# FFN block products on plain activations that accumulate in PSUM, three of seven with both activation parts in one product

## The chip, the core and the metric

The kernel runs on one core of one Trainium2 chip. Its time is the device time of one execution in microseconds (us); lower is better. The core has TensorE (PE in the profile; its weight loads are PEld), VectorE (DVE), ScalarE (ACT), GpSimd (POOL), SyncE (SP) and 16 DMA engines. Matmul results land in PSUM, a buffer of 8 banks of 512 fp32 columns on 128 partitions.

## The reference

A trunk of two residual layers on x, 512 frames by 1024 channels in fp32. Each layer is FFN, mixer, FFN; the first layer's mixer is an SSD and S5 pair, the second's a band attention and a pooling. The FFNs are most of the work:

```python
h = _rmsnorm(x, ffn1_norm[layer])
x = x + 0.5 * _swiglu(h, ffn1_w_gate[layer], ffn1_w_up[layer], ffn1_w_down[layer])

def _rmsnorm(x, gain):
    y = xf * lax.rsqrt(jnp.mean(xf * xf, axis=-1, keepdims=True) + EPS)
    return (y * gain)
def _swiglu(h, w_gate, w_up, w_down):
    return (jax.nn.silu(h @ w_gate) * (h @ w_up)) @ w_down
```

`w_gate` and `w_up` are 1024 by 2816, `w_down` is 2816 by 1024.

## The kernel before

**Stages.** f0 (FFN), even (SSD and S5), f1 (FFN), f2 (FFN), odd (attention and pooling), f3 (FFN), in this order, on one core. Activations lie transposed: 8 tiles of 128 channels by 512 frames.

**Products.** Every operand is split in two parts of a reduced fp32 format (`fp32r`): a high part, and the rest. A product is three matmuls: high weights by high activations, high weights by low activations, low weights by high activations. `split` makes a high part by a cast on ScalarE and a low part by a subtraction on VectorE. The tiles are `raw` (weights as loaded, 128x1024), `whl` (both parts of 1024 columns), `wh` (both parts of 512 columns), `hg` (both parts of 512 frames of activations).

**An FFN's gate and up products.** The 2816 hidden channels are 11 pairs q of two 128-channel tiles. Up to a limit (`CLASSIC`: q = 9 in f0, q = 3 in the others) they are classic: for each tile 8 products of 512 frames, on activations that are multiplied by the norm's gain only; the norm's factor per frame (`rsB`) is multiplied in when the result is taken out of PSUM (`evac`). From the limit on, `pair` makes the two tiles of gate (i = 0) or of up (i = 1) with seven block products instead of eight, after Strassen and Winograd. The frames are halved (columns 0 to 255 and 256 to 511), the channels that are summed over are halved, and the two tiles are the halves of the output. A block product is four steps of 128 channels, each three matmuls of 256 columns. Its inputs are blocks of weights (W1, which holds two, W3 with two sums, W4 with two sums, W2), and blocks of activations: N, the normalised ones, and TA and TB, sums and differences of them. `blocks` prepares these once per FFN: it normalises (`normed`), forms four sums per step, splits them, then normalises again and splits N in the place of the plain activations. `HOLD` says how many are kept in between. PE may not start the first pair before all of N and TB are there.

**`pair` before.** X takes two block products of W1 in its two halves, Y two of W3, Z two of W4, V one of W2; each half is a group of its own. ScalarE copies one half of X out (tile `p`), VectorE joins the seven with seven additions of 256 columns into `gs` (gate) or `us` (up), with intermediate sums in `u`.

**What follows.** Silu on ScalarE, gate times up on VectorE, split (`gate`), then the down products: units ("wdn") of 24 matmuls of 512 columns in four PSUM banks, added to x at the end of each of the four groups of q (`GROUPS`).

**The order of the work.** It is fixed when the program is written. `ffn_items` lists pairs and down units: a group's down units are spread between the next group's pairs, except that at the limit `LEAD` of them come first (3 in f1 to f3, 4 in f0; tables of two numbers stand in this order). A clock that models each engine (`Clock`) goes along; generators (the weight feeder, `evac`, `gate`, `blocks`, and in f0 the S5 preparation `s5_prepare`) are asked after each step of PE whether they are due, in an order of priority (`PRIO`), and issue an instruction once `on` finds its inputs due and the engine's backlog small. For PE, `SLACK` asks that inputs be ready some time earlier. `side` picks a PSUM buffer that the clock takes to be free. Semaphores make the engines wait for one another on the chip, whatever the clock said. Each engine runs its own instructions in the order written.

**Buffers.** Weight loads go through SyncE's queue into 3 `raw` buffers, and 3 more from the time when the S5 preparation is over; the pairs have 5 `whl` and 2 `wh`. PSUM has 4 buffers for projections and pairs (`b`) and 4 for down units (`a`).

Of the kernel before, what the change touches and what calls it, by code (L numbers as in the profile page):

```python
# [17 lines left out]
P = 128  # L18
# [23 lines left out]
CLASSIC = (3, 9)  # L42
LEAD = (3, 4)
HOLD = (1, 0)
# [11 lines left out]
PRIO = {"evac": 0, "gate": 0, "small": 5, "prep": 6, "blocks": 6, "s5_bounce": 1, "s5_quarter": 0, "s5_gate": 0, "s5_eighth": 1,  # L56
# [52 lines left out]
class Clock:  # L109
# [140 lines left out]
class Builder:  # L250
    def __init__(self, ctx, tc, A, out, plan):
# [18 lines left out]
        self.f, self.rsB, self.h, self.ndone, self.reserve, self.then, self.final = None, None, None, 0, 0, None, False  # L270
        self.xhold, self.go = False, False
# [24 lines left out]
    def add(self, kind, gen):  # L296
        p = PRIO[kind]
        i = next((i for i, (q, _) in enumerate(self.threads) if q >= p), len(self.threads))
# [19 lines left out]
    def on(self, eng, *aps, ps=0):  # L318
        c = self.clk
        while True:  # L320
            r = c.ready(*aps)
            if eng == "PE":
                ok = r + SLACK[self.name] <= c.now
# [4 lines left out]
            if ok and (not ps or self.side(ps) is not None):  # L328
                return
# [27 lines left out]
    def side(self, n=1):  # L357
# [387 lines left out]
    def ffn(self, f, gi, then, prepare=None):  # L745
# [4 lines left out]
        with ExitStack() as st:  # L750
# [7 lines left out]
            def extra():  # L758
# [4 lines left out]
                self.xhold, self.go = prep is None, False  # L763
# [3 lines left out]
            self.N, self.TA, self.TB, self.ndone = h, [], [], 0  # L767
            grown = False
            for key in ffn_items(f):
# [3 lines left out]
                if key[0] == "blocks":  # L773
# [4 lines left out]
                    self.go = True  # L778
# [20 lines left out]
                elif key[0] == "pair":  # L799
                    q, i = key[2:]  # L800
                    self.until(lambda: self.ndone == KD and len(self.TB) == 4)
                    if i == 0:
                        t = {"gs": self.pair(w, "gs")}
                        nc.scalar.activation(out=t["gs"], in_=t["gs"], func=AF.Silu)
                    else:
                        t["us"] = self.pair(w, "us")
                        self.add("gate", self.gate(t, g, q, [1] * 4, 1))
                        if q == NFF // 2 - 1:
                            self.give(*self.N, *self.TA, *self.TB)
                else:  # L810
# [8 lines left out]
                    if cg == 1:  # L819
                        self.give(g[2 * kp], g[2 * kp + 1])  # L820
            if grown:
# [16 lines left out]
    def evac(self, ps, t, tag, m, done):  # L838
        while not self.scaled():
            yield  # L840
        if t[tag] is None:
            yield from self.room(tag, 1)
            if t[tag] is None:
                t[tag] = self.ft.tile([P, 2, S], F32, tag=tag, name=self.n(tag), bufs=1)
            else:
                self.leave(tag)
# [22 lines left out]
    def blocks(self, h, gi, late):  # L869
# [5 lines left out]

        hold = HOLD[late]
        again, kept = range(max(0, 4 - hold)), {}

        def normalized(kk, tag):
            t = yield from self.grab(tag, F32)  # L880
            n = (t[:, 0], t[:, 1]) if tag == "hg" else (t[:, lo], t[:, hi])
            for i in range(2):
                yield from self.normed(n[i], 4 * i + kk, h, gi, late)
            return t, n

        for kk in range(4):
            tn, (n1, n2) = yield from normalized(kk, "raw" if kk in again else "hg")
# [7 lines left out]
            v.tensor_tensor(out=t4, in0=t2, in1=n2[:, a], op=ALU.subtract)  # L895
            if kk in again:
                self.give(tn)
            else:
                kept[kk] = tn, (n1, n2)
# [4 lines left out]
            self.give(rt)  # L904

        for kk in again[:2]:
# [1184 lines left out]
```

## Time and profile before

| | |
|---|---|
| median of 3 runs | 1813.72 us (1812.3 to 1814.33) |
| the profiled execution | 1810.71 us, its span 1808.7 us |
| mean granted TensorE clock | 0.999 |
| PE busy | 1792.4 us (99%) |
| DVE busy | 1428.9 us (79%) |
| ACT busy | 754.7 us (42%) |
| HBM read | 192.82 MB |

Nearly every instruction is recorded under one line of the kernel, that of a helper, so the rows are told apart by tiles: `ps<-hg,whl` is a matmul of activations and weights into PSUM. With 128x512 it is a classic or a down product, with 128x256 one of a block. `whl<-raw,whl` on DVE is the second half of a weight split. A row of a window gives, after its length, the busy us of PE, PEld, DVE, ACT and POOL with their instructions, then the granted clock, the DMA engines' busy share and GB/s. A row of a group gives busy us and the mean ns of one, then the engine's idle time before them and what ended it. The stages lie at: f0 from 0 to about 385 us, even to about 540, f1 and f2 to about 1245, odd to about 1405, f3 to the end.

### The profile page before, as it was taken

How to read it: one execution, taken by the hardware profiler on the slowest of the kernel's cores; microseconds unless marked ns; L12 is line 12 of the kernel's file. 1: busy time of each engine (PE TensorE's matmuls, PEld its weight loads, DVE VectorE, ACT ScalarE, POOL GpSimd, SP SyncE). 2: the span in 40 equal slices, each digit the busy share in tenths (PEclk: the TensorE clock that was granted, in tenths of full speed). 3: DMA queues.
4: the chain of work that ended last, by engine and by line, in shares of the span. 5: the costliest groups of instructions: out<-in, count | busy, mean ns of one | idle time of the engine just before them, and what ended most of it. 6: DMA issues, size and time to landing. Idle time of an engine off the chain costs nothing.

```text
span 1808.7 us, 26795 instructions
## 1 busy us (share of the span) xinstructions
PE 1792.4 (99%) x10514; PEld 1564.3 (86%) x10514; DVE 1428.9 (79%) x2599; ACT 754.7 (42%) x1082; POOL 18.7 (1%) x35
## 2 busy tenths in 40 slices
PE   9999999999999999999999999999999999999999
PEld 7877888978878889999988999998888788999997
DVE  8989877878986878887777988775578678988864
ACT  4323423433574444343343444333466544434331
POOL 0000000000010000000000000000000000000000
PEclk9999999999999999999999999999999999999999
DMA  5247432337773223332422333332434422333331
GB/s 196 92 141 190 144 103 82 117 130 205 201 168 114 88 89 104 118 105 95 138 64 78 106 117 97 103 102 86 144 78 111 129 82 76 100 106 107 111 98 70
DMA packets 80749, 207.16 MB, mean 115 GB/s; under 512 B 18000, under 2 KB 30320, under 8 KB 79472
## 3 DMA queue, kind: packets, MB, share of 16 engines
q1 hardware_dynamic: 78032, 196.52, 34.6%
q0 software_dynamic: 2448, 8.91, 3.1%
q8 instruction: 83, 1.36, 0.3%
q14 instruction: 42, 0.34, 0.1%
q10 hardware_dynamic: 144, 0.02, 0.0%
HBM read 192.82 MB, written 12.60 MB: 114 GB/s over the span
## 4 chain that ended last, share of the span: by engine, by line
PE 88%; DVE 8%; DMA 2%; issue 1%; ACT 1%; SPq 0%; DVEq 0%; ACTq 0%
PE ps L205 88%; DVE whl L205 1%; DVE hg L205 1%; DVE us L205 1%; DVE ex L205 1%; DVE ssb L205 1%; DMA raw<-in_wglu_dram 0%; DMA prm<-prm 0%; DMA s5ys<-ys 0%; ACT whl L205 0%; DVE s5x L205 0%; DMA ssb<-acsd 0%; DVE sc L205 0%; ACT hg L205 0%; DMA raw<-in_wgu_dram 0%
## 5 line engine op out<-in xcount | busy, mean ns | idle before, releaser
L205 PE MATMUL ps<-hg,whl 128*128 128x512 f32 (+1 forms) x8688 | 1609.6, 345 | 5.5 <-DVE hg L205 2.5
L205 PEld LDWEIGHTS ps<-hg,whl 128*128 128x128 f32 x8688 | 1375.5, 190 | 203.8 <-issue 4.6
L205 ACT CAST whl<-raw 128x1024 fp32r<-128x1024 f32 x366 | 383.0, 1051 | 532.3 <-PE ps L205 323.4
L205 DVE TENSOR_TENSOR whl<-raw,whl 128x1024 fp32r<-128x1024 f32 x349 | 424.1, 1222 | 180.8 <-ACT whl L205 180.3
L205 DVE SCALAR_TENSOR_TENSOR x<-ps,x 128x512 f32<-128x512 f32 x128 | 87.1, 688 | 37.0 <-PE ps L205 35.4
L205 DVE TENSOR_TENSOR raw<-raw,raw 128x512 f32<-128x512 f32 (+1 forms) x182 | 111.3, 649 | 2.2
L205 ACT CAST hg<-us 128x512 fp32r<-128x512 f32 x88 | 52.1, 620 | 105.2 <-DVE us L205 104.9
L205 PE MATMUL ps<-hg,wh 128*128 128x256 f32 x624 | 83.4, 283 | 0.0
L205 ACT ACTIVATE gs<-gs 128x1024 f32<-128x1024 f32 x44 | 46.7, 1060 | 85.5 <-DVE gs L205 85.5
L205 PEld LDWEIGHTS ps<-hg,wh 128*128 128x128 f32 x624 | 78.6, 192 | 0.0
L205 DVE TENSOR_TENSOR raw<-raw 128x512 f32<-128x512 f32 (+1 forms) x78 | 46.6, 597 | 16.4 <-DMA raw<-in_wgu_dram 16.4
L205 ACT COPY p<-ps 128x256 f32<-128x256 f32 x52 | 19.3, 372 | 95.5 <-PE ps L205 86.1
L205 DVE TENSOR_TENSOR hg<-us,hg 128x512 fp32r<-128x512 f32 x88 | 57.9, 685 | 0.0
L205 DVE TENSOR_TENSOR us<-gs,us 128x1024 f32<-128x1024 f32 x44 | 53.6, 1219 | 0.4
L205 ACT ACTIVATE hg<-x,gains 128x512 fp32r<-128x512 f32 x48 | 33.6, 722 | 32.4 <-DVE x L205 30.0
L205 ACT CAST hg<-raw 128x512 fp32r<-128x512 f32 x58 | 34.4, 622 | 21.3 <-DVE raw L205 20.6
L205 DVE TENSOR_TENSOR hg<-raw,hg 128x512 fp32r<-128x512 f32 x58 | 38.1, 689 | 0.1
L205 DVE SCALAR_TENSOR_TENSOR hg<-x,gains,hg 128x512 fp32r<-128x512 f32 x48 | 34.9, 746 | 2.5 <-ACT hg L205 2.5
L205 DVE TENSOR_TENSOR wh<-raw,wh 128x512 fp32r<-128x512 f32 x52 | 35.7, 686 | 0.0
L205 DVE TENSOR_TENSOR us<-ps,rsB 128x512 f32<-128x512 f32 x40 | 28.9, 723 | 4.5 <-PE ps L205 4.4
L205 ACT CAST wh<-raw 128x512 fp32r<-128x512 f32 x52 | 32.0, 616 | 0.0
L205 DVE TENSOR_TENSOR acc<-acc,sq 128x512 f32<-128x512 f32 x42 | 29.0, 690 | 0.9
(264 smaller groups left out, 1100.0 us busy)
## 6 DMA issues: line engine op xcount, KB each, us to landing
raw<-in_wgu_dram SPq DMA_DIRECT2D x176, 512.0 KB, 3.6
raw<-in_wdn_dram SPq DMA_DIRECT2D x88, 512.0 KB, 3.6
raw<-in_wev_dram SPq DMA_DIRECT2D x16, 512.0 KB, 3.6
prm<-prm SPq DMA_DIRECT2D x8, 1024.0 KB, 6.9
raw<-in_wod_dram SPq DMA_DIRECT2D x12, 512.0 KB, 3.6
raw<-in_wevo_dram SPq DMA_DIRECT2D x8, 512.0 KB, 6.6
raw<-in_wodo_dram SPq DMA_DIRECT2D x8, 512.0 KB, 6.4
x<-in_xT_dram SPq DMA_DIRECT2D x8, 256.0 KB, 5.6
```

The costliest lines, as they stand in the source:

```text
L205: r = f(*args, **kw)
```

## The change

`blocks` no longer normalises in the end: N is the plain activations (gain only), whose two parts exist already. TA and TB are still made of normalised values. `pair` multiplies the results of products on N by `rsB` when it takes them out of PSUM (`times`), as `evac` does. Three block products (W3 by TA, W4 by TB, W2 by TB) and one on N are now read from buffers that go on growing: Y takes W3's, is read, takes W4's on top of it (no fresh start), is read, takes W2's, is read; so sums that VectorE had made are made by accumulation. X takes W1's first block, is read, takes the second on top. Before such a block, PE waits until VectorE has read what stands there. The sign of one sum in `blocks` (t4) is turned round for it. `WIDE` is true for all FFNs: in Y's three blocks, high weights meet both parts of the activations in one matmul of 512 columns (two runs of 256 in `hg`), high by high in columns 0 to 255 and high by low in columns 256 to 511; VectorE then adds both halves (`plus`). The low weights by high follow in columns 0 to 255. W2's block (`last`) is put off: it is issued after the down unit that follows, or inside the next pair behind its first two blocks. Each pair has 12 operations of VectorE on 256 columns, and ScalarE's copy is gone.

Besides: q = 8 of f0 is a pair too, no down units are put ahead of the pairs (`LEAD`), threads of equal priority except `evac` go in as before and `evac` behind its equals, `blocks` gets priority 0, the clock's price of an `fp32r` matmul of n columns is (n + 32) / 2400, and the slack for an operand holds for the PSUM buffer too, with 4 us for the products of the S5 preparation (`PREP_SLACK`).

```diff
-CLASSIC = (3, 9)
-LEAD = (3, 4)
-HOLD = (1, 0)
+CLASSIC = (3, 8)
+LEAD = (0, 0)
+WIDE = (True, True)
...
+PREP_SLACK = 4.0
-PRIO = {"evac": 0, "gate": 0, "small": 5, "prep": 6, "blocks": 6, ...
+PRIO = {"evac": 0, "gate": 0, "small": 5, "prep": 6, "blocks": 0, ...
...
-                return max(0.11, 0.0025 + n / 2400)
+                return (n + 32) / 2400
...
-            ok = min(most - self.open[w], sum(t <= self.clk.now for t in self.freed[w]))
+            ok = min(most - self.open[w], sum(t + slack <= self.clk.now for t in self.freed[w]))
...
-            v.tensor_tensor(out=t4, in0=t2, in1=n2[:, a], op=ALU.subtract)
+            v.tensor_tensor(out=t4, in0=n2[:, a], in1=t2, op=ALU.subtract)
...
-        for kk in (3, 2, 1, 0):
-            if kk not in kept:
-                kept[kk] = yield from normalized(kk, "raw")
-            for i in range(2):
-                yield from self.split_steps(n[i], h[4 * i + kk])
...
+    def block(self, ps, t, at, rhs, c, more=False, wide=False):
         for kk in range(4):
+            self.until(lambda: len(rhs) > kk)
             w = slice(at + kk * P, at + kk * P + P)
             r = rhs[kk]
+            first, last = kk == 0 and not more, kk == 3
+            o = ps[:, 0:256]
+            go = dict(start=first, stop=False, skip_group_check=more)
+            if wide:
+                nc.tensor.matmul(out=ps.rearrange("p (a b) -> p a b", a=2), lhsT=t[:, 0, w], rhs=r[:, :, c], **go)
+            else:
+                nc.tensor.matmul(out=o, lhsT=t[:, 0, w], rhs=r[:, 0, c], **go)
+                go["start"] = False
+                nc.tensor.matmul(out=o, lhsT=t[:, 0, w], rhs=r[:, 1, c], **go)
+            nc.tensor.matmul(out=o, lhsT=t[:, 1, w], rhs=r[:, 0, c], start=False, stop=last, skip_group_check=more)
             self.tick()
...
+        def plus(out, ps, x):
+            add(out, ps[:, lo], x)
+            if wide:
+                add(out, ps[:, hi], out)
         X = self.main_ps()
+        self.block(X, W1, 0, N[0:4], lo)
+        p1 = new("p1", 2)
+        times(p1, X[:, lo], lo)
+        Z = self.main_ps()
+        self.block(Z[:, hi], W4, 512, N[4:8], hi)
+        if before:
+            before()
+        t[tag] = dst = self.ftile(tag)
+        Y = self.main_ps()
+        self.block(Y, W3, 512, TA, hi, wide=wide)
+        plus(dst[:, 0, hi], Y, p1)
+        self.block(X, W1, 512, N[4:8], lo, more=True)
+        times(dst[:, 0, lo], X[:, lo], lo)
+        self.block(Z, W3, 0, TA, lo)
+        add(dst[:, 0, hi], Z[:, lo], dst[:, 0, hi])
+        times(p5, Z[:, hi], hi)
+        add(dst[:, 0, hi], dst[:, 0, hi], p5)
+        self.block(Y, W4, 0, TB, lo, more=True, wide=wide)
+        plus(dst[:, 1, hi], Y, p1)
+        add(dst[:, 1, hi], Z[:, lo], dst[:, 1, hi])
+        def last():
+            self.block(Y, W2, 0, TB, hi, more=True, wide=wide)
+            plus(dst[:, 1, lo], Y, p1)
```

**Where instructions moved.** PE in a pair of f1, from the end of Y's first wide block to the start of its second (`ps_6065` is Y, `ps_6028` X, `ps_6050` Z; four `hg` tiles per block):

```order
L207 MATMUL ps_6065<-hg_5622,whl_5946 128x512
L207 MATMUL ps_6065<-hg_5622,whl_5946 128x256
L207 MATMUL ps_6028<-hg_5316,whl_5882 128x256 x3
L207 MATMUL ps_6028<-hg_5331,whl_5882 128x256 x3
L207 MATMUL ps_6028<-hg_5340,whl_5882 128x256 x3
L207 MATMUL ps_6028<-hg_5374,whl_5882 128x256 x3
L207 MATMUL ps_6050<-hg_5516,whl_5946 128x256 x3
L207 MATMUL ps_6050<-hg_5560,whl_5946 128x256 x3
L207 MATMUL ps_6050<-hg_5605,whl_5946 128x256 x3
L207 MATMUL ps_6050<-hg_5622,whl_5946 128x256 x3
L207 MATMUL ps_6065<-hg_5534,whl_5964 128x512
```

A wide step is one matmul of 512 and one of 256 columns; 24 products of 256 stand between Y's two blocks.

VectorE in a pair of f1 before: seven additions one behind the other (`ps_6355`, `ps_6398`, `ps_6425`, `ps_6453` are X, Y, Z, V), then splits of weights:

```order
L205 TENSOR_TENSOR us_6396<-ps_6355,p_863_6352 128x256
L205 TENSOR_TENSOR u_864_6353<-ps_6398,p_863_6352 128x256
L205 TENSOR_TENSOR us_6396<-ps_6398,u_864_6353 128x256
L205 TENSOR_TENSOR u_865_6354<-ps_6425,u_864_6353 128x256
L205 TENSOR_TENSOR us_6396<-ps_6398,u_865_6354 128x256
L205 TENSOR_TENSOR us_6396<-ps_6425,us_6396 128x256
L205 TENSOR_TENSOR us_6396<-u_865_6354,ps_6453 128x256
L205 TENSOR_TENSOR whl_6393<-raw_6318,whl_6393 128x1024
```

And the pair of the change whose PE rows stand above, up to the additions that Y's last block waits for:

```order
L207 TENSOR_TENSOR p_825_6048<-ps_6028,rsB_5473 128x256
L207 TENSOR_TENSOR whl_6046<-raw_5991,whl_6046 128x1024
L207 TENSOR_TENSOR us_6064<-ps_6065,p_825_6048 128x256
L207 TENSOR_TENSOR us_6064<-ps_6065,us_6064 128x256
L207 TENSOR_TENSOR us_6064<-ps_6028,rsB_5473 128x256
L207 TENSOR_TENSOR whl_6092<-raw_6010,whl_6092 128x1024
L207 TENSOR_TENSOR us_6064<-ps_6050,us_6064 128x256
L207 TENSOR_TENSOR p_830_6105<-ps_6050,rsB_5473 128x256
L207 TENSOR_TENSOR us_6064<-us_6064,p_830_6105 128x256
L207 TENSOR_TENSOR whl_6110<-raw_6034,whl_6110 128x1024
L207 TENSOR_TENSOR us_6064<-ps_6065,p_825_6048 128x256
L207 TENSOR_TENSOR us_6064<-ps_6065,us_6064 128x256
```

Splits of weights now stand between the additions, one ahead of each pair of additions that reads Y.

PE in f0 at the first small products of the S5 preparation (`ident,bt` and `s5bm`), before:

```order
L205 MATMUL ps_1042<-ident,bt_963 128x128 x4
L205 MATMUL ps_1049<-g_107_971,s5bm 32x128 x4
L205 MATMUL ps_1014<-hg_206,whl_914 128x512 x3
L205 MATMUL ps_1078<-g_111_983,s5bm 32x128 x4
L205 MATMUL ps_1014<-hg_215,whl_914 128x512 x3
```

And now:

```order
L207 MATMUL ps_995<-ident,bt_919 128x128 x4
L207 MATMUL ps_1002<-hg_589,whl_880 128x512 x3
L207 MATMUL ps_974<-hg_634,whl_880 128x512 x3
L207 MATMUL ps_1017<-g_101_927,s5bm 32x128 x4
L207 MATMUL ps_981<-hg_634,whl_880 128x512 x3
L207 MATMUL ps_988<-hg_634,whl_880 128x512 x3
L207 MATMUL ps_1048<-g_103_935,s5bm 32x128 x4
```

Six products of 512 columns stand between the groups where there were none and three, and they fall inside a down unit instead of a gate or up tile.

More of the change, by code (lines that the diff above doesn't have):

```diff
@@ L269, in __init__ @@
         self.raws, self.ahead = [], []
[L270 to L271 removed]
+        self.f, self.rsB, self.h, self.reserve, self.then, self.final = None, None, None, 0, None, False
+        self.xhold = False
         self.later = []
@@ L297, in add @@
         p = PRIO[kind]
-        i = next((i for i, (q, _) in enumerate(self.threads) if q >= p), len(self.threads))
+        i = next((i for i, (q, _) in enumerate(self.threads) if q > p or q == p and kind != "evac"), len(self.threads))
         self.threads.insert(i, (p, gen))
@@ L322, in on @@
             if eng == "PE":
-                ok = r + SLACK[self.name] <= c.now
+                ok = r + slack <= c.now
             elif eng == "DMA":
@@ L327, in on @@
                 ok = r <= c.now + 0.3 and c.t[eng] <= c.now + self.backlog
-            if ok and (not ps or self.side(ps) is not None):
+            if ok and (not ps or self.side(ps, slack) is not None):
                 return
@@ L800, in ffn, with pending @@
                     q, i = key[2:]
-                    self.until(lambda: self.ndone == KD and len(self.TB) == 4)
                     if i == 0:
[L803 to L809, printed above, removed]
+                        t = {}
+                    last = self.pair(w, t, "us" if i else "gs", pending)
+                    def pending(last=last, t=t, q=q, i=i):
+                        last()
+                        if i == 0:
+                            nc.scalar.activation(out=t["gs"], in_=t["gs"], func=AF.Silu)
+                        else:
+                            self.add("gate", self.gate(t, g, q, [1] * 4, 1))
+                            if q == NFF // 2 - 1:
+                                self.give(*self.N, *self.TA, *self.TB)
                 else:
@@ L840, in evac @@
             yield
+        while t[tag] is None and self.cnt.get(tag, 0):
+            yield
         if t[tag] is None:
[L842 to L846, printed above, removed]
+            self.cnt[tag] = 1
+            t[tag] = self.ft.tile([P, 2, S], F32, tag=tag, name=self.n(tag), bufs=1)
         yield from self.on("DVE", ps, self.rsB)
@@ L874, in blocks @@
             yield
[L876 to L881, printed above, removed]
-            for i in range(2):
-                yield from self.normed(n[i], 4 * i + kk, h, gi, late)
-            return t, n
         for kk in range(4):
-            tn, (n1, n2) = yield from normalized(kk, "raw" if kk in again else "hg")
+            tn = yield from self.grab("raw")
+            n1, n2 = tn[:, lo], tn[:, hi]
+            for i, n in enumerate((n1, n2)):
+                yield from self.normed(n, 4 * i + kk, h, gi, late)
             rt = yield from self.grab("raw")
@@ L939, in pair @@
         N, TA, TB = self.N, self.TA, self.TB
-        add = lambda out, x, y, op=ALU.add: v.tensor_tensor(out=out, in0=x, in1=y, op=op)
-        p1, u2, u3 = (self.ft.tile([P, 256], F32, tag=tag, name=self.n(tag), bufs=1) for tag in ("p1", "u2", "u3"))
-        X = self.main_ps()
-        a = self.block(X[:, lo], W1, 512, N[4:8], lo)
-        self.block(X[:, hi], W1, 0, N[0:4], lo, a)
+        add = lambda out, x, y: v.tensor_tensor(out=out, in0=x, in1=y, op=ALU.add)
+        times = lambda out, x, c: v.tensor_tensor(out=out, in0=x, in1=self.rsB[:, c], op=ALU.mult)
@@ L974, in gate @@
+        return last
     def gate(self, t, g, q, ready, done):
@@ L1175, in gains_of_outputs @@
             yield from self.on("DVE")
-            yield from self.on("PE", g1, bmx, ps=1)
+            yield from self.on("PE", g1, bmx, ps=1, slack=PREP_SLACK)
             psk = self.side_ps()
@@ L1212, in gains_of_inputs @@
             v.tensor_tensor(out=bt, in0=bt, in1=tb, op=ALU.add)
-            yield from self.on("PE", bt, ps=1)
+            yield from self.on("PE", bt, ps=1, slack=PREP_SLACK)
             pst = self.side_ps()
```

70 lines of the change are left out of this document (19 added, 51 removed).

## The prediction

> **What bounds the kernel now.** I began with the page: busy shares, slices, and the chain that ended last.
>
> ```profile
> span 1808.7 us, 26795 instructions
> PE 1792.4 (99%) x10514; PEld 1564.3 (86%) x10514; DVE 1428.9 (79%) x2599; ACT 754.7 (42%) x1082; POOL 18.7 (1%) x35
> PEclk9999999999999999999999999999999999999999
> PE 88%; DVE 8%; DMA 2%; issue 1%; ACT 1%; SPq 0%; DVEq 0%; ACTq 0%
> ```
>
> TensorE (PE) is busy 99% of the span and makes 88% of the chain. Matmul ends are modelled, so this alone doesn't say that it streams without gaps. Two more views do: everything PE waited for (kind, total, times, longest), and three of the four FFNs in windows (from 560 us the second and third, from 1420 the last).
>
> ```profile
> PE ps L205 <- DVE hg L205: 3.0, 3, 1.5
> PE ps L205 <- DVE us L205: 2.9, 1, 2.9
> PE ps L205 <- DVE ones L205: 1.1, 1, 1.1
> PE ps L205 <- DVE whl L205: 1.1, 2, 0.5
> 560.00:1240.00 680.00, 680.00 (x4253) 617.34 (x4252) 541.95 (x822) 273.49 (x348) 0.00 (x0) 1.00 0.33 101
> 1420.00:1800.00 380.00, 380.00 (x2343) 342.36 (x2342) 287.47 (x434) 147.85 (x190) 0.00 (x0) 1.00 0.30 96
> ```
>
> In these 1060 us PE (the second column) is busy to the last hundredth, and its long waits come to 8.1 us in all; none of the others lasts 1 us. So a us of matmul removed from an FFN is a us of the span, as long as what feeds PE keeps up. The feeder is VectorE (DVE, the fourth column), 541.95 of 680 us busy.
>
> What does a matmul cost on PE? Not its mean duration (283 or 392 ns, which includes the pipeline), but the step from start to start. The timeline merges equal instructions; the start of the next piece gives the step.
>
> ```profile
> 559.75 27.37 PE L205 MATMUL ps<-hg,whl 128*128 128x512 f32 x120
> 586.96 0.95 PE L205 MATMUL ps<-ones,acc 128*128 128x1 f32 x8
> ...
> 739.79 6.76 PE L205 MATMUL ps<-hg,whl 128*128 128x256 f32 x55
> 746.39 1.60 PE L205 MATMUL ps<-hg,wh 128*128 128x256 f32 x12
> ```
>
> 512 columns: (586.96 - 559.75) / 120 = 226.8 ns. 256 columns: (746.39 - 739.79) / 55 = 120.0 ns. Two of 256 cost 240.0 ns, one of 512 costs 226.8: 13.2 ns less for the same columns. Half of 226.8 is 113.4, so a step has a fixed part of about 13 ns.
>
> **The change, part by part.**
>
> ```profile
> L205 PE MATMUL ps<-hg,whl 128*128 128x256 f32 x3744 | 457.4, 283 | 0.0
> L205 PE MATMUL ps<-hg,wh 128*128 128x256 f32 x624 | 83.4, 283 | 0.0
> ```
>
> Matmuls: 3744 + 624 = 4368 block products are 52 pair units of 84 (7 blocks x 4 x 3). A unit is now 4 blocks of 12 x 120.0 ns (5.76 us) and 3 wide blocks of 4 x (226.8 + 120.0) ns (4.16 us): 9.92 us, against 84 x 120.0 ns = 10.08. The first FFN turns q=8 from classic into two more units: 54. PE before: 52 x 10.08 = 524.2 us, plus that q's 96 classic products, 96 x 226.8 ns = 21.8 us. After: 54 x 9.92 = 535.7. The term is -10.3 us.
>
> A product whose moving operand is two runs of 256 is nowhere in the trace. Its bounds: 226.8 ns (one run of 512) and 240.0 (each run pays the fixed part). I take 226.8, since the columns go by at the same pace in both rows and the fixed part goes with the instruction. At 240.0 the term shrinks to 54 x 10.08 - 524.2 - 21.8 = -1.7 us.
>
> The Trainium skill (TensorE: Matmul & The Clock Gate, "Back-to-back issue gap") speaks against this term: there a warm step is N/2.4 + 2.5 ns, 109.2 and 215.8 ns, so that a wide product would save 2.5 ns, and the same sum gives an estimated -4.0 us. The trace has 120.0 and 226.8, a fixed part five times as large, and the measurement decides.
>
> The one long stall: in the first FFN, where the S5 preparation slips its small products in.
>
> ```profile
> 97.40 0.96 PE L205 MATMUL ps<-hg,whl 128*128 128x512 f32 x3
> 101.22 0.42 PE L205 MATMUL ps<-g,s5bm 128*32 128x128 f32 x8 [2.86 <-DVE us L205]
> ...
> 99.75 0.69 DVE L205 TENSOR_TENSOR hg<-us,hg 128x512 fp32r<-128x512 f32 x1
> 100.47 0.69 DVE L205 TENSOR_TENSOR us<-ps,rsB 128x512 f32<-128x512 f32 x1
> ...
> 101.30:104.70 3.40, 3.40 (x15) 2.56 (x16) 3.16 (x21) 2.08 (x5) 0.00 (x0) 0.54 0.66 231
> ```
>
> The second group waits 2.86 us for an evacuation that frees its PSUM buffer (DVE ends it at 101.16, PE starts at 101.22). Then the granted clock is 0.54 for 3.40 us, which loses 3.40 x 0.46 = 1.6 us: 4.4 us in all. The change asks 4 us of slack for the operands and the buffer of these groups, more than the 2.86, and PE's order puts six products where three were. I count -4.4; bounds 0 (the wait comes back) and -4.4.
>
> The Trainium skill agrees on the second half (same page, "HAM oscillation"): a PE idle for a window of about 3.4 us drops to half clock; here 2.86 us of wait were enough.
>
> Waiting longer makes the preparation end later. It ends by 190 us, and then 510 products of 226.8 ns, 116 us, come before the first pair; the earlier pair takes about half of that. Cost nothing; if the cover were gone, PE would wait for the remainder.
>
> ```profile
> 190.00:400.00 210.00, 0.00 (x0) 0.00 (x0) 0.00 (x0) 1.00 0.35 113
> L205 PE MATMUL ps<-hg,whl 128*128 128x512 f32 x510 | 116.4, 390 | 0.2 <-DVE x L205 0.2
> ```
>
> DVE: the normalised activations are no longer made and split, but each pair unit has 12 additions or multiplications of 256 instead of 7, and ScalarE loses its copy. Does DVE still feed PE? The pair stage of the second FFN stage (16 units, 660 to 898 us), in four windows, with its rows:
>
> ```profile
> 660.00:720.00 60.00, 60.00 (x464) 58.32 (x463) 53.06 (x85) 25.43 (x34) 0.00 (x0) 1.00 0.31 98
> ...
> sum 238.00, PE 238.00 PEld 224.48 DVE 190.11 ACT 93.03 POOL 0.00; mean PE 59.50 PEld 56.12 DVE 47.53 ACT 23.26 POOL 0.00
> L205 DVE TENSOR_TENSOR us<-ps,u 128x256 f32<-128x256 f32 x16 | 6.8, 425 | 0.5
> DVE whl L205 <- ACT whl L205: 26.3, 23, 4.7
> DVE us L205 <- ACT p L205: 5.8, 6, 1.8
> DVE gs L205 <- ACT p L205: 4.2, 2, 3.2
> ```
>
> 80 more operations of 425 ns make 190.1 + 34.0 = 224.1 us of DVE in 238 - 16 x 0.16 = 235.4 us of PE: 95%. It fits, just. The 10.0 us of waits for ScalarE's copy go with the copy.
>
> The new tight places: X and Y now grow in one PSUM buffer, so PE may not go on adding to it until DVE has read it. Behind Y's first block come 24 products (2.88 us) before W4's block adds to Y, behind X's first block 12 products and a wide block (2.83 us). A waiting matmul holds up everything on PE. DVE has to do the two additions there, and by the order a weight split ahead of them: 2 x 0.425 + 1.22 = 2.07 us, under 2.88. W2's block comes after a whole down unit, 24 x 226.8 ns = 5.44 us. So I count 0 for all pairs; bounds 0 and, if a second split (1.22 us) stood in the way each time, 54 x (3.29 - 2.88) = +22 us.
>
> ```profile
> L205 DVE TENSOR_TENSOR whl<-raw,whl 128x1024 fp32r<-128x1024 f32 x63 | 76.3, 1222 | 26.3 <-ACT whl L205 26.3
> ```
>
> Weights: W1's buffer is now held until three narrow blocks and a wide one are through (3 x 1.44 + 1.39 = 5.7 us instead of 2.9), W2's until a down unit has passed. The next unit's W3 takes W1's buffer, and is wanted 2.9 us into that unit, whose period is 9.92 + 5.44 = 15.4 us: 12.5 us are left for a cast of 1.05 and a split of 1.22. Cost 0; without that cover PE would wait 2.3 us a pair. SyncE issues as many weight loads as before, only with down weights and pair weights in turn, and the DMA engines are a third busy (0.33 in the window from 560 us).
>
> ```profile
> L205 ACT CAST whl<-raw 128x1024 fp32r<-128x1024 f32 x366 | 383.0, 1051 | 532.3 <-PE ps L205 323.4
> ```
>
> The rest: the shorter build-up ahead of the pairs, the even order of the down units, and the threads' new order of insertion lie beside a PE that has no waits in the FFNs: 0. In the mixers (385 to 540 us, 1245 to 1420) the order shifts too; PE's busy time there leaves 4.8 and 1.3 us, so I allow 3 us either way.
>
> ```profile
> 385.00:540.00 155.00, 150.19 (x931) 122.29 (x930) 133.39 (x342) 80.44 (x138) 7.79 (x9) 1.00 0.69 187
> 1245.00:1420.00 175.00, 173.74 (x955) 142.59 (x954) 127.09 (x289) 96.41 (x185) 10.12 (x20) 1.00 0.38 98
> ```
>
> Sum: -10.3 - 4.4 = -14.7 us. The profiled execution took 1810.71 us, 2.0 more than its span; it becomes 1796.0. The three timed runs have their median, 1813.72, 3.0 us above the profiled execution; the same distance gives **1799.0 us**.
>
> **The rivals.**
> Two runs cost as much as two products: PE gains 1.7 instead of 10.3, 1813.7 - 1.7 - 4.4 = 1807.6 us. For it: no row has such an operand. Against: the fixed part looks like one per instruction.
>
> By the skill's page above, with its fixed part of 2.5 ns, the estimate would be 1805 us.
>
> The stall at 98 us stays, or turns up at another of the small groups: 1813.7 - 10.3 = 1803.4 us. For it: that whole passage is reordered, and DVE is the late one there. Against: 4 us of slack against 2.86 late.
>
> DVE becomes the bound in the pair stages: the slower side. If DVE goes on waiting 26.3 us for ScalarE's casts there, its 224.1 us become 250.4 in a stage where PE needs 235.4: +15.0 us in each of the last three FFNs, 1813.7 - 14.7 + 45.0 = 1844 us. The place is PE at Y's W4 block, and it decides once DVE is more than 2.88 us late; 14.7 / 54 = 0.27 us of stall per pair would eat the gain. Against: a DVE with older work queued reaches a split after its cast has ended, so these waits shrink as the load grows.
>
> The mixers' new order sheds half of their idle time as well: 1796 us.
>
> **How the numbers follow.** Forecast 0.58 (its own range 1794 to 1804: 3 us of the mixers, and up to 2 of small stalls); two runs cost double 0.10; the stall stays 0.15; DVE bound 0.10; mixers gain too 0.07. About 0.2% (3.6 us) is what the timing can tell from no change. Faster than 1810.1: nearly all of the first, second, third and last case, 0.85. Within: 0.06, from the edges and a mild DVE case. Slower than 1817.3: 0.09. A range of 1793 to 1811 holds all but the DVE case and the outer edges.
>
> **What would show it.** Right: the timeline of a pair stage with rows of 512 and 256 whose starts give 4.16 us for a wide triple; PE without waits for DVE between the second FFN and the end; no 2.86 us wait and no 0.54 clock near 98 us; DVE near 95% in the pair stage. Wrong: waits of PE for `gs` or `us` on DVE in each pair, a PE busy share that falls there, or a step of 240 ns for the wide product.

## The result, and the profile after

The changed kernel takes **1895.01 us** (median of 4 runs, 1893.85 to 1896.39), the kernel before 1813.01 (4 runs, 1812.17 to 1814.33): 1.0445 times as long, 95% interval 1.043 to 1.046. The forecast was 1799.0 us and faster. It was wrong by 96 us, and in its sign. One execution of a run below (e4) took 2524 us at a mean granted clock of 0.65; it is left out of that run's median.

The page of the kernel after: span, busy time, granted clock by slices, and the chain by engine.

```profile
span 1894.7 us, 25720 instructions
PE 1818.5 (96%) x9938; PEld 1547.3 (82%) x9938; DVE 1496.9 (79%) x2824; ACT 721.4 (38%) x1002; POOL 18.6 (1%) x35
PEclk9999999999999899999998999999999989999999
PE 65%; DVE 23%; issue 5%; DMA 4%; ACT 3%; SPq 0%; DVEq 0%; ACTq 0%
```

PE's busy share falls from 99 to 96%, three slices show a lower clock, and VectorE (DVE) has 23% of the chain instead of 8%. DVE's busy share of the span is the same 79%: on the whole it is not short of time. What PE waited for (total, times, longest), the two largest entries, tells more:

```profile
PE ps L207 <- DVE gs L207: 37.5, 21, 4.3
PE ps L207 <- DVE us L207: 21.4, 3, 7.1
```

Of 58.9 us, 21.4 come in three waits of 7.1, one in each of the last three FFNs. So it is not every pair that is late; something happens once per FFN. Windows of the kernel after find it: the stretch of classic products ahead of the first pair, in the second, third and last FFN, and between them the pair stage of the second FFN.

```profile
598.00:655.00 57.00, 40.39 (x150) 31.67 (x149) 34.00 (x55) 15.29 (x19) 0.00 (x0) 0.85 0.19 65
655.00:940.00 285.00, 283.13 (x1689) 251.79 (x1688) 240.49 (x396) 98.76 (x114) 0.00 (x0) 1.00 0.32 104
975.00:1025.00 50.00, 33.38 (x113) 25.79 (x112) 26.29 (x43) 10.97 (x16) 0.00 (x0) 0.80 0.18 53
1535.00:1585.00 50.00, 33.38 (x115) 25.82 (x114) 26.60 (x43) 12.55 (x17) 0.00 (x0) 0.80 0.16 53
```

All products in the three short windows have 512 columns, 226.8 ns each at full clock. 150 of them are 34.0 us of work in 57: 23.0 lost. 113 are 25.6 in 50: 24.4 lost. 115 are 26.1: 23.9 lost. Together **71.3 us**, most of the 82. The pair stage, where the rival saw the danger, loses 1.9 us of PE's busy time in 285.

What happens there, on PE's timeline of the kernel after (start, length, instruction, wait before it):

```profile
608.28 7.31 PE L207 MATMUL ps<-hg,whl 128*128 128x512 f32 x24 [3.66 <-DVE gs L207]
622.72 7.25 PE L207 MATMUL ps<-hg,whl 128*128 128x512 f32 x24 [7.12 <-DVE us L207]
634.30 13.69 PE L207 MATMUL ps<-hg,whl 128*128 128x512 f32 x48 [4.33 <-DVE gs L207]
649.49 5.69 PE L207 MATMUL ps<-hg,whl 128*128 128x512 f32 x24 [1.50 <-DVE gs L207]
```

24 products are one tile's projection. Before each row PE waits for DVE to take an earlier tile out of PSUM. The waits sum to 16.6 us; the rest of the 23 is lowered clock behind them. What DVE does before the longest one, on its own timeline:

```profile
611.71 0.42 DVE L207 TENSOR_TENSOR raw<-raw,raw 128x256 f32<-128x256 f32 x1
616.75 1.23 DVE L207 TENSOR_TENSOR whl<-raw,whl 128x1024 fp32r<-128x1024 f32 x1 [4.62 <-ACT whl L207]
617.89 1.29 DVE L207 TENSOR_TENSOR hg<-raw,hg 128x512 fp32r<-128x512 f32 x2
619.10 1.41 DVE L207 SCALAR_TENSOR_TENSOR raw<-x,gains,rsB 128x512 f32<-128x512 f32 x2
620.42 0.42 DVE L207 TENSOR_TENSOR raw<-raw 128x256 f32<-128x256 f32 x1
...
621.88 0.68 DVE L207 TENSOR_TENSOR us<-ps,rsB 128x512 f32<-128x512 f32 x1
```

The evacuation `us<-ps,rsB` that PE needs comes last, at 621.88. Ahead of it stand a weight split, two splits of TA and TB, two normalisations and four sums: all of `blocks`, except the weight split. And that split waits 4.62 us for a cast on ScalarE, whose row says why:

```profile
615.67 1.04 ACT L207 CAST whl<-raw 128x1024 fp32r<-128x1024 f32 x1 [8.62 <-PE ps L207]
```

The cast starts when PE is through with the 24 products that end at 615.59 (608.28 + 7.31) and so frees a weight buffer. PE then waits for a PSUM buffer, which waits for an evacuation, which stands in DVE's queue behind the split, which waits for the cast. From 615.59 on the cast, the split, 4.0 us of `blocks` and the evacuation follow one another: these are PE's 7.12 us. The work of `blocks` is 4 x (1.41 + 4 x 0.42 + 1.29) = 17.5 us wherever it stands; its place ahead of the evacuations makes it a stall.

### The profile page after: what moved, and what is told of

Read it like the earlier page. It is cut to its first block, busy times and chain, and to the rows that moved or that the text cites. A ratio compares the mean times of both kernels' runs of the same rounds, so it can differ in the third digit from the quotient of the medians.

```text
span 1894.7 us, 25720 instructions
## 1 busy us (share of the span) xinstructions
PE 1818.5 (96%) x9938; PEld 1547.3 (82%) x9938; DVE 1496.9 (79%) x2824; ACT 721.4 (38%) x1002; POOL 18.6 (1%) x35
## 4 chain that ended last, share of the span: by engine, by line
PE 65%; DVE 23%; issue 5%; DMA 4%; ACT 3%; SPq 0%; DVEq 0%; ACTq 0%
PE ps L207 65%; DVE whl L207 5%; DVE us L207 4%; DVE raw L207 3%; DMA raw<-in_wgu_dram 3%; ACT whl L207 2%; DVE hg L207 1%; DVE gs L207 1%; DVE x L207 1%; DVE s_t L207 1%; DVE wh L207 1%; DVE ct L207 1%; DVE p L207 1%; DVE ex L207 0%; DMA raw<-in_wev_dram 0%
## 5 line engine op out<-in xcount | busy, mean ns | idle before, releaser
L207 PE MATMUL ps<-hg,whl 128*128 128x512 f32 (+1 forms) x8304 | 1631.6, 356 | 64.9 <-DVE gs L207 37.5
L207 PEld LDWEIGHTS ps<-hg,whl 128*128 128x128 f32 x8304 | 1358.8, 191 | 291.3 <-issue 53.4
L207 PE MATMUL ps<-hg,wh 128*128 128x512 f32 (+1 forms) x432 | 84.5, 338 | 0.0
L207 PEld LDWEIGHTS ps<-hg,wh 128*128 128x128 f32 x432 | 69.9, 188 | 11.4
L207 DVE TENSOR_TENSOR gs<-ps,gs 128x256 f32<-128x256 f32 x135 | 57.2, 423 | 3.7
L207 DVE TENSOR_TENSOR us<-ps,us 128x256 f32<-128x256 f32 x135 | 57.1, 423 | 3.7
L207 DVE TENSOR_TENSOR us<-ps,p 128x256 f32<-128x256 f32 x81 | 34.0, 420 | 22.3 <-PE ps L207 22.3
L207 DVE TENSOR_TENSOR gs<-ps,p 128x256 f32<-128x256 f32 x81 | 34.0, 420 | 15.1 <-PE ps L207 13.3
L207 DVE TENSOR_TENSOR p<-ps,rsB 128x256 f32<-128x256 f32 x108 | 44.9, 416 | 0.0
L207 DVE TENSOR_TENSOR us<-ps,rsB 128x512 f32<-128x512 f32 (+1 forms) x65 | 39.0, 600 | 6.6 <-PE ps L207 6.3
```

The costliest lines, as they stand in the source:

```text
L207: r = f(*args, **kw)
```

## The experiments

All times are medians; ratios are to the kernel before on the same chip in the same batch (its medians there: 1811.85 to 1813.06 us), with 95% intervals.

| run | what it is | us | ratio to before |
|---|---|---|---|
| e1 | change, `blocks` at priority 6 again | 1823.46 | 1.0061 [1.0046, 1.0076] |
| e2 | change, former rule of insertion | 1823.08 | 1.0063 [1.0045, 1.0082] |
| e3 | before, with the change's priority and rule | 1848.65 | 1.0201 [1.0177, 1.0225] |
| e4 | e1, no wide products | 1822.10 | 1.0063 [1.0043, 1.0083] |
| e5 | e1, more products between Y's blocks | 1815.83 | 1.0017 [1.0008, 1.0025] |
| e6 | e1, former price in the clock | **1808.79** | 0.9977 [0.9967, 0.9988] |
| e7 | e1, former slack | 1827.05 | 1.0076 [1.0060, 1.0091] |
| e8 | e1, wide operand in one run | 1821.10 | 1.0044 [1.0030, 1.0058] |
| e9 | change, former price | 1854.76 | 1.0234 [1.0218, 1.0250] |
| e10 | e6, no wide products | 1812.45 | 1.0000 [0.9991, 1.0009] |
| e11 | e1, small backlog in f1 to f3 | 1813.61 | 1.0001 [0.9992, 1.0010] |
| e12 | before, new price | 1822.95 | 1.0059 [1.0045, 1.0073] |
| g1 | change, small backlog in f1 to f3 | 1868.98 | 1.0318 [1.0302, 1.0334] |
| g2 | e6, small backlog in f0 | 1814.82 | 1.0013 [1.0004, 1.0022] |

**The queue ahead of the evacuations: e1, e2, e3.** The expectations call the reading above Q. L and W are the rivals that look for the cause in the new pairs themselves (their load on VectorE; their wide products and weight buffers); by them the order of `blocks` would change little.

```diff
 e1
-PRIO = {... "blocks": 0, ...}
+PRIO = {... "blocks": 6, ...}
 e2
-        i = next((i for i, (q, _) in enumerate(self.threads) if q > p or q == p and kind != "evac"), len(self.threads))
+        i = next((i for i, (q, _) in enumerate(self.threads) if q >= p), len(self.threads))
 e3: the kernel before, with "blocks": 0 and the rule that e2 takes out
```

> The changed kernel with one number turned back: the preparation of the activation blocks has the last priority (6) again instead of the first (0). Theory Q (queue): ahead of the pairs of each of the last three FFNs, the evacuations of the classic products stand on VectorE behind the blocks' operations and behind weight splits that wait for PE; PE runs out of PSUM buffers, waits 3.7, 7.1, 4.3 and 1.5 us and loses more to a lowered clock, about 24 us per FFN. Then the evacuations come first again and 3 x 24 = 72 us go: 1823 us, between 1818 and 1828, and no wait of PE over 2 us there. Rival L (load): VectorE has too much to do with five more operations a pair, whatever the order; then the time stays above 1880. Rival W (wide): the products of 512 columns are slow; then it stays above 1880 too.

> The changed kernel with the other half of the ordering turned back: threads of equal priority go in front, evacuations too; the blocks keep priority 0. Theory Q: what matters is that an evacuation is asked ahead of the blocks, so this alone removes the same stalls: 1823 us, between 1818 and 1830. If the blocks' priority itself matters (they take the engine's time from gates and splits too), it lands between 1830 and 1880. Rivals L and W: above 1880.

> The kernel before with the two ordering edits alone: blocks at priority 0 and evacuations behind their equals. Its products and additions are those of before. Theory Q: the stalls come without any of the new products, some 40 to 90 us: 1855 to 1900 us. Rivals L and W: no change, 1810 to 1818 us.

e1 and e2 each undo one half and each takes away 72 us (1895.0 to 1823.5 and 1823.1), the 71.3 of the three windows. It takes both: `blocks` at the priority of the evacuations, and evacuations put behind their equals. The stretch in e1, DVE's timeline (three evacuations; what lies between them is left out):

```profile
607.43 0.69 DVE L207 TENSOR_TENSOR us<-ps,rsB 128x512 f32<-128x512 f32 x1
...
613.63 0.68 DVE L207 TENSOR_TENSOR gs<-ps,rsB 128x512 f32<-128x512 f32 x1
...
618.68 0.68 DVE L207 TENSOR_TENSOR us<-ps,rsB 128x512 f32<-128x512 f32 x1
```

An evacuation every 5 to 6 us, and PE's timeline there is one unbroken row. (A row merges neighbours with the same tiles and names the shape of the first; this one runs on into the first pair, from 648.24 us.)

```profile
597.70 58.57 PE L207 MATMUL ps<-hg,whl 128*128 128x512 f32 x283
```

e3 puts the same two edits into the kernel before, with none of the new pairs: 36 us slower than before (two executions, 1845.77 and 1851.54). The direction is Q's and excludes L and W as the cause of these stalls, the size is below Q's range (1855). Its waits in the second FFN:

```profile
605.88 7.31 PE L205 MATMUL ps<-hg,whl 128*128 128x512 f32 x24 [3.13 <-DVE gs L205]
617.59 19.37 PE L205 MATMUL ps<-hg,whl 128*128 128x512 f32 x72 [4.40 <-DVE us L205]
640.26 5.04 PE L205 MATMUL ps<-hg,whl 128*128 128x512 f32 x14 [3.30 <-DVE gs L205]
```

Three stalls of 10.8 us instead of four of 16.6, and one of the three FFNs has none. So something else in the change makes the same order worse; e9 finds most of it below.

**What e1 still loses: e4 to e8.** e1 is 10.4 us slower than before, although its matmuls take 7 us less (see e8). I added up, for each stage, by how much the distance from one matmul's start to the next exceeds the usual step (226.8 or 120.0 ns). Against the kernel before, e1 has some 12 us more in the pairs of f1 to f3 and some 7 us more in f0 and the mixers. The pairs: PE's and DVE's timelines of e1 around one of the longer stalls.

```profile
835.12 7.33 PE L207 MATMUL ps<-hg,whl 128*128 128x256 f32 x56
843.35 7.12 PE L207 MATMUL ps<-hg,whl 128*128 128x512 f32 x32 [0.90 <-DVE gs L207]
```
```profile
838.55 0.69 DVE L207 TENSOR_TENSOR raw<-raw 128x512 f32<-128x512 f32 x1 [0.68 <-DMA raw<-in_wgu_dram]
839.28 1.90 DVE L207 TENSOR_TENSOR raw<-raw,raw 128x512 f32<-128x512 f32 x3
841.09 1.22 DVE L207 TENSOR_TENSOR us<-gs,us 128x1024 f32<-128x1024 f32 x1
842.41 0.42 DVE L207 TENSOR_TENSOR gs<-ps,p 128x256 f32<-128x256 f32 x1
842.87 0.42 DVE L207 TENSOR_TENSOR gs<-ps,gs 128x256 f32<-128x256 f32 x1
```

PE waits at the block of 512 that grows in Y for `gs<-ps,gs`, which ends at 843.29. Ahead of it stand four sums of weights and the multiplication of gate by up, 3.8 us, not the one split that the prediction counted. There are 48 such places in f1 to f3. Counted by starts, PE is late at 15 of them by over 0.1 us, 1.7 at most and 9.8 in sum.

```diff
 e4  -WIDE = (True, True)
     +WIDE = (False, False)
 e5  Z's block of W4 by N moves behind Y's first block:
     -        Z = self.main_ps()
     -        self.block(Z[:, hi], W4, 512, N[4:8], hi)
              if before: before()
              t[tag] = dst = self.ftile(tag)
              Y = self.main_ps()
              self.block(Y, W3, 512, TA, hi, wide=wide)
              plus(dst[:, 0, hi], Y, p1)
     +        Z = self.main_ps()
     +        self.block(Z[:, hi], W4, 512, N[4:8], hi)
 e6  -                return (n + 32) / 2400
     +                return max(0.11, 0.0025 + n / 2400)
 e7  -yield from self.on("PE", ..., ps=1, slack=PREP_SLACK)
     +yield from self.on("PE", ..., ps=1)
     -sum(t + slack <= self.clk.now for t in self.freed[w])
     +sum(t <= self.clk.now for t in self.freed[w])
 e8  -matmul(out=ps.rearrange("p (a b) -> p a b", a=2), lhsT=..., rhs=r[:, :, c], **go)
     +matmul(out=ps, lhsT=..., rhs=r[:, 0, :], **go)
```

> As the first of these, blocks last, and all block products narrow: no product of 512 columns in the pairs, 84 of 256 a unit, and VectorE has three additions less in each. Against the first of these it prices the wide product. If a wide product steps at 226.8 ns, as I predicted, 648 x 13.2 ns = 8.6 us are lost: 1831 us beside 1823. The trace of the changed kernel has a step of 235 ns from a product of 512 to one of 256 and 118 back, so that 353 to 355 ns stand for 360: 3 to 5 us lost, 1827 us. If two runs cost as much as two products: no difference, or a little faster since VectorE has less to do.

> e1 (blocks at priority 6) with one thing moved in the pair: Z's block of W4 by plain activations (12 products, 1.44 us) goes behind Y's first block, so that 4.3 us of products instead of 2.9 lie between Y's two wide blocks; X's gap stays. Lateness theory: what e1 still loses in the pair stages is PE waiting for VectorE at Y's second block, at most 1.7 us at a time, so with 1.4 us more of cover nearly all of the 11 us of such waits goes: 1812 to 1815 us. Load theory: VectorE is too busy there on the whole, and the wait comes back at another block of the pair: 1819 to 1824 us.

> e1 with the clock's former price of a product (0.11 us for 256 columns, 0.2158 for 512, instead of 0.120 and 0.2267). If the price is what shifted the first FFN and the even mixer (6.6 us more idle in e1 than before), 1816 to 1819 us; if not, 1822 to 1825. A clock that thinks PE faster than it is issues VectorE's work relatively later in PE's order, so the waits in the pairs could also change: up to 5 us either way.

> e1 without the 4 us of slack for the S5 preparation and without slack for PSUM buffers (as before). If these caused the idle time at 89 to 97 us and in the even mixer, 1818 to 1821 us; if the 2.9 us stall of before comes back in its place, no difference: 1822 to 1825.

> e1, but the wide products read one run of 512 columns (the high part of all frames) instead of two runs of 256 (so these three block products are not the ones wanted; number, size and buffers of all operations are as in e1). If the 8 ns that a wide product costs beyond 226.8 come from its two runs, its step falls from 235 to 227 and the time by 54 x 12 x 8 ns = 5 us: 1818 to 1819 us. If they come from the alternation of 512 and 256 columns, the step stays 235 and the time 1822 to 1825.

e5 gains 7.6 us over e1 with nothing changed but the distance between Y's first two blocks, and PE has no wait left in that pair stage. That is most of the 12, and the time lies just above the 1812 to 1815 of the lateness theory: lateness at that block, not load.

e6 gains more, 14.7 us, by putting the clock's price back. That was expected to be worth 4 to 7, give or take 5 for the pairs; it is more than the two together. At the 48 places PE is late by 0.2 us in sum, and its pair stage in the second FFN has no wait of PE (the sum of four windows, 660 to 898 us):

```profile
sum 238.00, PE 238.00 PEld 214.35 DVE 209.52 ACT 86.40 POOL 0.00; mean PE 59.50 PEld 53.59 DVE 52.38 ACT 21.60 POOL 0.00
```

e6 is the fastest version of the study and 0.23% faster than before. e7 is 3.6 us slower than e1, above both of its expectations, though the intervals of the two ratios overlap. A wait of 2.97 us is back in it, at 87 us. So the added slack is not the cause of what e1 loses; it may be a help.

e4 against e1: no difference, the last of its cases. Its expectation takes that to mean that two runs cost as much as two products, but there is another reading. Without wide products PE has more to do and DVE less, and the waits at Y shrink by about as much. e8 and e10 decide between the two.

e8 settles what a wide product costs. Its wide products read the high part of all 512 frames in one run, so it leaves out the low part and its results are not the ones wanted; the number and size of all operations are e1's. A block whose weights are in a `wh` tile is four triples of 512 and 256 columns alone in a row of PE's timeline. First e1, then e8:

```profile
662.26 1.56 PE L207 MATMUL ps<-hg,wh 128*128 128x512 f32 x8
663.66 4.62 PE L207 MATMUL ps<-hg,whl 128*128 128x256 f32 x33
```
```profile
664.33 1.56 PE L207 MATMUL ps<-hg,wh 128*128 128x512 f32 x8
665.73 6.49 PE L207 MATMUL ps<-hg,whl 128*128 128x256 f32 x49
```

From start to start 1.40 us in both. Two runs cost nothing more than one run, and the block takes less than the 1.44 us of twelve narrow products. e8 as a whole is 2.4 us faster than e1, with overlapping intervals and without a difference in these steps, so I read nothing into it. By 4 x (226.8 + 120.0) it should be 1.387, by narrow products it is 1.44. The other two wide blocks of a pair, which follow a product of 256, take 1.41 in the median of the trace. So a pair unit is 4 x 1.44 + 1.40 + 2 x 1.41 = 9.98 us instead of 9.92, and the matmul term 54 x 9.98 - 524.2 - 21.8 = **-7.1** instead of -10.3. The missing part belongs to the alternation of 512 and 256 columns; what it is in the array stays open.

**The clock's price: e9 to e12, g1, g2.**

```diff
 e9   the change with   return max(0.11, 0.0025 + n / 2400)
 e10  e6 with           WIDE = (False, False)
 e11  e1 with           BACKLOG = {... "f1": 0.8, "f2": 0.8, ... "f3": 0.8}    (1.5 each before)
 e12  before with       return (n + 32) / 2400
 g1   the change with e11's BACKLOG
 g2   e6 with           BACKLOG = {"f0": 1.5, ...}    (2.5 before)
```

> The change as it was (blocks at priority 0, evacuations inserted behind their equals), with one thing put back: the clock's former price of a product. Queue theory: the stalls ahead of the pairs come from the priority, the price only adds the waits in the pairs, so this is the e6 time plus the 72 us that e1 took away: 1870 to 1890 us. Price theory: a clock whose PE is a little too fast leaves VectorE enough room for both, and the stalls ahead of the pairs don't build up: under 1830.

> e6 (blocks at priority 6, former price) with narrow products everywhere in the pairs: three products of 256 in place of one of 512 and one of 256, and no second addition behind them. PE has no waits left in e6's pairs, so the wide triple's measured gain, 360 - 353 = 7 ns in 54 x 12 triples, is lost in full: 4.5 us, 1812 to 1814 us. If VectorE's shorter work gives something back, no difference: 1807 to 1811.

> e1 with the former price NOT put back, but VectorE's allowed backlog in f1 to f3 reduced from 1.5 to 0.8 us. If the former price helps in the pairs since less work is queued on VectorE ahead of a pair's own additions, this does the same: the 11 us of pair waits shrink by 6 or more, 1812 to 1818 us. If it helps by other means (due times of weights), 1820 to 1826.

> The kernel before with the new price of a product alone. If the price shifts the first FFN and the mixers by itself, they lose about what they lost in e1 (5 to 8 us) and the pairs, whose PSUM buffers don't wait for VectorE there, nothing: 1817 to 1822 us. If the price hurts only with the new pairs, no difference: 1811 to 1815.

> The change as it was (priority 0, new price), with VectorE's allowed backlog in f1 to f3 at 0.8 instead of 1.5 us. Length theory: the stalls ahead of the pairs come from how much work lies on VectorE ahead of an evacuation, whoever puts it there; then a short backlog alone takes away most of the 72 us, and the 11 us in the pairs as well: 1812 to 1835 us. Order theory: the threads of blocks go first whatever the backlog is, each evacuation still comes behind four normalisations and the split that waits for ScalarE: 1865 to 1890.

> e6 with VectorE's allowed backlog in the first FFN at 1.5 instead of 2.5 us. If the two stalls left there (2.6 us at 98 and 2.1 us at the first pair, 254 us) are evacuations that lie behind queued work, they go: 1804 to 1806 us. If VectorE has too much to do there on the whole, no difference or a loss: 1808 to 1812.

Priority and price make a square:

| | former price | new price | difference |
|---|---|---|---|
| `blocks` at 6 | 1808.8 (e6) | 1823.5 (e1) | 14.7 |
| `blocks` at 0 | 1854.8 (e9) | 1895.0 (the change) | 40.2 |
| difference | 46.0 | 71.5 | |

e9 lies between its two expectations: the two causes make each other worse. With the former price the stalls ahead of the pairs are there, but shorter (e9, PE's timeline):

```profile
609.31 7.20 PE L207 MATMUL ps<-hg,whl 128*128 128x512 f32 x24 [3.13 <-DVE gs L207]
620.92 19.27 PE L207 MATMUL ps<-hg,whl 128*128 128x512 f32 x73 [4.40 <-DVE us L207]
```

These are nearly e3's first two stalls; e3 has the former price too. The third FFN, which has none in e3, has such stalls in e9 (8.1 and 3.9 us of waits for `gs` and `us` from 930 to 1020 us). At this price the order costs 46.0 us in the change (e9 against e6) and 36.2 in the kernel before (e3). What makes the other 10 was not tested: `LEAD`, the pair at q = 8 and the new pairs themselves were not turned back apart.

e12: the new price alone makes the kernel before 10 us slower, 1 us above the expected range. By the same count of starts none of it is in the FFNs from f1 on; it is in f0 and the even mixer. The longest waits are now for an S5 operand, up to 2.9 us again:

```profile
PE ps L205 <- DVE bt L205: 5.2, 3, 2.9
```

The new price is the truer one: by the quoted steps 256 columns take 120.0 ns, and it says 120; the former says 110. The clock's truth is not what made the order good. A clock that prices PE's products 5 to 8% too low (0.2158 for 0.2268, 0.110 for 0.120) would let DVE's work in later for each step of PE, so that less of it lies queued when a pair's own additions come. e11 tests this with the price left alone and a smaller allowance for DVE's queue: 9.9 us faster than e1, the pair waits nearly gone (1.8 us at the 48 places), as expected. The DVE work that lies between the end of Y's first block and its first addition comes to at most 4.0 us in e1, 2.6 in e11 and 2.1 in e6. So in the pairs it is the length of DVE's queue, and both edits shorten it.

Ahead of the pairs it is not only that. g1, with the small allowance and the change's order, keeps most of its loss (1869.0, at the lower end of the order theory). PE's timeline, and DVE's before the first stall:

```profile
616.29 7.82 PE L207 MATMUL ps<-hg,whl 128*128 128x512 f32 x24 [4.60 <-ACT hg L207]
628.70 13.86 PE L207 MATMUL ps<-hg,whl 128*128 128x512 f32 x48 [4.60 <-ACT hg L207]
```
```profile
611.42 1.41 DVE L207 SCALAR_TENSOR_TENSOR raw<-x,gains,rsB 128x512 f32<-128x512 f32 x2
612.85 1.23 DVE L207 TENSOR_TENSOR whl<-raw,whl 128x1024 fp32r<-128x1024 f32 x1
613.99 0.42 DVE L207 TENSOR_TENSOR raw<-raw 128x256 f32<-128x256 f32 x1
...
615.46 0.69 DVE L207 TENSOR_TENSOR us<-ps,rsB 128x512 f32<-128x512 f32 x1
```

The evacuation `us<-ps,rsB` again comes behind `blocks` and a split. (The profile puts PE's wait down to a cast of ScalarE that ends about when this evacuation does, at 616.15; PE starts at 616.29.) The circle is there too: DVE's waits for a weight's cast from 598 to 655 us, in the change, in g1 and in e1.

```profile
DVE whl L207 <- ACT whl L207: 22.1, 3, 9.0
```
```profile
DVE whl L207 <- ACT whl L207: 18.8, 5, 7.9
```
```profile
DVE whl L207 <- ACT whl L207: 6.4, 3, 3.0
```

So here it is the order; the length of the queue only sets the size. Of the change's 82 us, g1's backlog takes 26: some 8 at Y's blocks (PE is late there by 9.7 us in the change, 1.6 in g1), and the rest from shorter stalls (4.6 + 4.6 + 1.5 = 10.7 us in this FFN instead of 16.6, and the clock behind them). That the former price shortens the stalls of e9 in the same way is likely, but wasn't tested apart.

e10 against e6: wide products are worth 3.7 us here (the intervals of the two ratios don't touch), where the rows give 54 x 0.10 = 5.4. With them goes all that the change gains: e10 is level with before.

g2: 6 us slower than e6. By the count of starts f0 gains some 6 us, as expected, and the even mixer behind it loses some 12. A smaller queue in one stage moves the order of all that follows; the expectation, made from f0 alone, was too narrow.

## Why the prediction was wrong

- **The step that failed** is "The rest: the shorter build-up ahead of the pairs, the even order of the down units, and the threads' new order of insertion lie beside a PE that has no waits in the FFNs: 0." That PE had no waits there was a fact of the old order, which put evacuations first, and the step took it as a reserve. The new priority of `blocks` stands in none of its terms. The new order cost 71.5 us (e1, e2), in the very stretch where PE needs a PSUM buffer every 5.4 us. The cover that should have been named is that evacuations precede `blocks` in DVE's queue. The order of DVE's instructions in that stretch could be read beforehand: sixteen instructions of `blocks` and a weight split between two evacuations. I had looked at the order inside the pairs only.
- **The clock's price** was not costed at all. It took 14.7 us in e1, 10 in the kernel before, and 40 together with the new order.
- **The matmul term** was right in kind: -10.3 forecast, -7.1 by the rows. Mis-sized was the wide block, 1.40 to 1.41 us against 1.387. The rival that two runs cost as much as two products is excluded by e8.
- **The rival by the Trainium skill** (TensorE: Matmul & The Clock Gate, "Back-to-back issue gap"): by its step of N / 2.4 + 2.5 ns a wide triple would save 2.5 ns. The trace shows (1.44 - 1.40) / 4 = 10 and (1.44 - 1.41) / 4 = 7.5 ns, between the Trainium skill's 2.5 and the 13.2 of the rows of before; the term of -7.1 lies halfway between -4.0 and -10.3.
- **The f0 stall**, -4.4: it moved, as that rival said, to 2.14 us at 96 us in the kernel after, without the loss of clock behind it, with smaller waits beside it. Of the 4.4 nothing was left: f0 has some 3 us more idle time in e1 than before. Without the slack e7 is 3.6 us slower still, with overlapping intervals.
- **DVE in the pair stage**: forecast 224.1 us of 235.4 (95%); e6, with PE unbroken, has 209.5 of 238 (88%). A pair starts every 15.4 us there, so the window holds some 15 of them and not the 16 of the forecast. It fits, as said, and the rival by which it becomes the bound there was right in its sign and wrong in place and cause. Its counter-argument held: the 26.3 us of waits for ScalarE's cast shrank, to 9.2 in e6.
- **The tight place at Y's W4 block** was named rightly, with 2.88 us of cover, and costed at 0. It is 0.2 us in f1 to f3 under the former price (e6) and 9.8 under the new (e1), most of the 12 that e1 loses in the pairs. The list of what stands ahead on DVE was too short.
- **The weights' buffers**, cost 0: in the pairs no wait of PE for a weight shows in the kernel after. Right.

The account: -7.1 for matmuls, some 12 in the pairs and 7 in f0 and the mixers (12 together, where e1 measured 10.4; the price makes 14.7 of the 19), 71.5 from the order. That is 83 against 82.0. With order and price put back, e6 gains 4.3 of the 14.7 us forecast. Of the 10.4 that are missing, 3.2 are the wide blocks, 4.4 the f0 stall that brought nothing, and by the count of starts the rest, some 3, lies in f0 and the mixers; its cause was not tested.

## What to carry to other kernels

"The bound engine has no waits here" is a property of the order that is about to be changed; before costing a new priority at nothing, read the order of the engine that feeds it and count what now stands between two of the instructions that free its buffers. A scheduler's cost model is part of a tuned kernel even where it is wrong: a truer price can cost more than a structural edit gains, and belongs in a run of its own. When a change bundles a structural gain with scheduling edits, undo the latter one by one: here the gain was 7 us of matmuls, 4 us of the whole time with the others put back, and a priority, a rule of insertion and a price hid it.

## What the runs showed of the hardware

A wait of PE can cost clock as well as itself. Windows of 3.40 us behind waits of 1.50 and 4.33 us in the kernel after; the granted clock is the third number from the end:

```profile
649.49:652.89 3.40, 3.40 (x15) 2.84 (x16) 3.37 (x5) 0.67 (x2) 0.00 (x0) 1.00 0.24 92
634.30:637.70 3.40, 3.40 (x8) 2.73 (x9) 0.45 (x1) 0.94 (x1) 0.00 (x0) 0.50 0.23 89
```

The length of the wait alone doesn't decide. In the kernel after, a wait of 1.81 us (1240.66 to 1242.47) is followed by half the clock; in e9 one of 3.73 us (999.73 to 1003.46) is not:

```profile
1240.41:1243.83 3.42, 1.61 (x10) 1.25 (x9) 3.28 (x6) 2.09 (x3) 0.00 (x0) 1.00 0.00 0
1243.83:1247.24 3.41, 3.41 (x10) 2.68 (x9) 3.31 (x9) 1.56 (x2) 0.00 (x0) 0.50 0.51 154
```
```profile
998.18:1001.60 3.42, 1.55 (x7) 0.94 (x5) 3.38 (x6) 1.86 (x3) 0.00 (x0) 1.00 0.34 127
1001.60:1005.01 3.41, 1.55 (x7) 1.32 (x8) 3.41 (x6) 0.00 (x0) 0.00 (x0) 1.00 0.44 142
1005.01:1008.42 3.41, 3.41 (x17) 2.83 (x16) 0.10 (x1) 0.00 (x0) 0.00 (x0) 1.00 0.03 12
```

In all 16 traces the granted clock changes only at points that lie a multiple of 3.41 us apart within a run, and these windows begin and end at such points. The short wait lies whole in one window, the long one is split over two. So where a wait falls seems to matter. It isn't the whole rule: PE's busy time in the windows with the wait is nearly the same, 1.61 and 1.55 us. What decides stays open.

At the low clock a product of 512 columns takes 3.40 / 8 = 0.425 us, not twice 226.8 ns: the fixed part of about 13 ns at full clock is not there. The Trainium skill (TensorE: Matmul & The Clock Gate, "Back-to-back issue gap") gives N / 1.2 GHz for that state, 426.7 ns, and the trace agrees; at full clock its N / 2.4 + 2.5 ns, 215.8, does not meet the 226.8 here.
